# A token tile of 1024 instead of 512, weights always cast on load, and a sample group kept feature-major, in one decoder step on eight cores

## The chip, the cores and the metric

The kernel runs on all 8 cores of one Trainium2 chip (two dies of four cores). Each core does the same program on its own share of the batch; there is no traffic between cores. The metric is the device time of the slowest core in microseconds (us). Executions of one kernel mostly agree within 0.3% (12 of the 15 runs of the kernel before lie that near to their median, and all 8 of the changed kernel); now and then a die falls into a slower state, at a lower granted TensorE clock (in a run of the kernel before that took 1528.1 us, 0.88 on the cores of one die against 0.97 on the other; no trace of a slow run was kept).

## The reference, cut to what matters

One decoder layer with width 1024, for two groups of tokens that use the same weights: a prompt group (per core 1 sequence of 2048 tokens) and a sample group (per core 16 sequences of 4 tokens, so 64 tokens, each sequence with its own recurrent state of 4 x 128 x 256 floats and its own cached keys and values of 256 memory tokens).

```python
def token_mix(xn, s0, buf, pos0, p):
    proj = xn @ p['w_in']
    q, k, v, gz, og, u, ga, gb = jnp.split(proj, split_points(), axis=-1)
    ...
    o, s_new = gla_chunked(q, k, v, log_a, s0)            # gated linear attention with a carried state
    o = rmsnorm(o, p['gla_norm_g']).reshape(B, T, GLA_VAL_W) * jax.nn.silu(og)
    branch_a = o @ p['w_branch_a']
    pooled, buf_new = pool_mix(u, buf, pos0, p['w_pool_mix'], p['pool_scale'])
    branch_b = pooled @ p['w_branch_b']
    merged = jax.nn.sigmoid(ga) * branch_a + jax.nn.sigmoid(gb) * branch_b
    return merged @ p['w_out'], s_new, buf_new

def decoder_layer(x, mk, mv, s0, buf, pos0, p):
    mix, s_new, buf_new = token_mix(rmsnorm(x, p['norm_mix_g']), s0, buf, pos0, p)
    h = x + mix
    h = h + cross_attn(rmsnorm(h, p['norm_x_g']), mk, mv, p['w_xq'], p['w_xo'])
    h = h + sq_relu_mlp(rmsnorm(h, p['norm_mlp_g']), p['w_up'], p['w_down'])
    return h, s_new, buf_new
```

All inputs are float32. The kernel's matmuls take bf16 operands.

## The kernel before: the parts that matter

The program is written as a list of operations per engine, which a scheduler in the kernel orders at build time. Weights come in units of 1024 x 512 (1 MB in bf16), each landing in a slot. `W(name)` hands out the next slot and starts its load: from the float32 weights with a cast on the way, or, where the same unit has been cast before, from a bf16 scratch in HBM.

```python
NSLOT = 5
NT = SEQ // 512                                  # four prompt tiles of 512 tokens
...
def W(self, name):
    ...
    if name in ONCE:
        cast, store = True, False
    elif name[:2] == "bp":
        cast, store = False, False
    elif times <= STORE_AT.get(name, 1):
        cast, store = True, times == STORE_AT.get(name, 1)
    else:
        cast, store = False, False
    if cast:
        self.dma("pool", flat, src, nb=5.0, ahead=60.0, after=...)
    else:
        self.dma("sp", flat, self.scr[idx], nb=2.5, rtok=[("scr", idx)], ahead=60.0)
    if store:
        self.dma("sp", self.scr[idx], flat, nb=2.5, wtok=[("scr", idx)])
    return u
```

The prompt is done tile by tile; each stage of a tile asks for a unit and uses it on all the tile's tokens. The sample group's 64 tokens are done beside it, whenever a unit that they need is in a slot, and in generators that the prompt's loops step forward (`self.step("G", 2)`). Two projections exist: `sfm` holds the weights still and streams 64 tokens, `stm` holds the tokens still and streams 512 weight columns.

```python
def sfm(self, u, srcT):                          # 32 matmuls of 64 columns
    b = self.bank()
    self.mms([(self.pb[b][:, m * 64:(m + 1) * 64], self.fm(u, m, srcT, 64)) for m in range(4)])
def stm(self, u, srcT):                          # 8 matmuls of 512 columns
    b = self.bank()
    self.mm(self.pb[b][:64, :], self.tm(u, 0, srcT, sp=64))
```

The carried states of the 16 sequences go through a ring of buffers. To get one sequence's four query rows against its own state while keeping 64 output rows, the queries sit in a window of zeros (`qw`):

```python
for i in range(SB):
    sf = self.ring(...)                                                    # float32 state
    self.dma("sp", sf[...], I["sgla"][i], nb=1.4)
    self.cp("act", sb_[:, :, :], sf[:, :, :])                              # bf16 copy, ScalarE
    self.cp("dve", qw[:, :, 60:64], self.qs[:, :, i * ST:(i + 1) * ST])
    self.ts("dve", kb[:, :], self.kdts[:, :], self.bmk[:, i:i + 1], ALU.mult, ...)
    for hp in range(2):
        self.mma([(self.pb[ob[hp]][:64, ...], [(qw[:, h, 60 - ST * i:124 - ST * i], sb_[:, h, :])]) for h in ...], ...)
        ...                                                                # state update, 64-row operands
    self.dma("sp", O["sgs"][i], sf[...], nb=1.4)
```

Of the kernel before, what the change touches and what calls it, by code (L numbers as in the profile page):

```python
# [19 lines left out]
SB = 16  # L20
# [4 lines left out]
NSLOT = 5  # L25
NT = SEQ // 512
# [416 lines left out]
def make_consts():  # L443
# [26 lines left out]
    mu = np.zeros((64, 4, 64), np.float32)  # L470
# [17 lines left out]
    bk = np.zeros((64, SB), np.float32)  # L488
# [9 lines left out]
for _n, _w in (("g_mix", 8), ("g_x", 8), ("g_mlp", 8), ("g_mem", 8), ("g_gla", 2), ("pscale", 8), ("bgk", 4)):  # L498
    COLS[_n] = (_o, _w)
    _o += _w  # L500
# [21 lines left out]
ONCE = ("xk0", "xk1", "xv0", "xv1", "b0", "b1", "xqT0", "xqT1", "xq0", "xq1", "xo0", "xo1")  # L522

STORE_AT = {f"up{i}": 0 for i in range(8)}
STORE_AT.update({f"dn{c}_{n}": 0 for c in range(4) for n in range(2)})
STORE_AT.update(dict.fromkeys(("og0", "og1", "u0", "u1"), 2))
# [15 lines left out]
class Fixed:  # L542
    def __init__(self, ap):
        self.ap = ap

# [12 lines left out]
class Prog:  # L558
    def __init__(self):
        self.nc = nc = bass.Bass("TRN2", target_bir_lowering=False)  # L560
# [9 lines left out]
        inp("xp", [SEQ, D]); inp("xs", [SB * ST, D]); inp("mem", [MEM, D])  # L570
# [6 lines left out]
        outp("yp", [SEQ, D]); outp("ys", [SB * ST, D]); outp("mk", [MEM, D]); outp("mv", [MEM, D])  # L577
# [3 lines left out]
        with contextlib.ExitStack() as stack:  # L581
# [3 lines left out]
            self.mark = {}  # L585
            for mode in ("count", "plan", "emit"):
# [22 lines left out]
                self.seen = {}  # L609
# [14 lines left out]
    def alloc(self):  # L624
# [5 lines left out]
        def reg(size, gran=256):  # L630
# [6 lines left out]
        self.ur = g.sb("ur", reg(10240), [128, 5, 1024], BF16)  # L637
        self.WqK = g.sb("WqK", reg(16384), [128, 8, 1024], BF16)
        self.VWo = g.sb("VWo", reg(16384), [128, 8, 1024], BF16)
        self.wt += [g.sb(f"wx{i}", g.byname[n] + o, [128, 8, 512], BF16)  # L640
                    for i, (n, o) in enumerate((("WqK", 0), ("WqK", 8192), ("VWo", 0), ("VWo", 8192)))]
        XH = reg(16384)
        self.xh = g.sb("xh", XH, [128, 4, 1024], F32)
        self.actT = g.sb("actT", reg(8192), [128, 8, 512], BF16)
        R = reg(16384)
        self.E1 = g.sb("E1", R, [128, 4, 512], F32)
        self.E2 = g.sb("E2", R + 8192, [128, 4, 512], F32)
        self.o2T = g.sb("o2T", R, [128, 8, 512], BF16)
        self.dT = g.sb("dT", R + 8192, [128, 8, 512], BF16)
        self.hid = [g.sb(f"hid{i}", R + 8192 * i, [128, 8, 512], BF16) for i in range(2)]  # L650
        Q = reg(24576)
        self.qi = g.sb("qi", Q, [128, 4, 512], BF16)
        self.kd = g.sb("kd", Q + 4096, [128, 4, 512], BF16)
        self.kdt = [g.sb(f"kdt{i}", Q + 8192 + 1024 * i, [128, 512], BF16) for i in range(2)]
        self.Sb = [g.sb(f"Sb{i}", Q + 10240 + 2048 * i, [128, 4, 256], BF16) for i in range(2)]
        self.T1 = g.sb("T1", Q, [128, 4, 512], F32)
        self.vt = g.sb("vt", Q + 14336, [128, 4, 1024], BF16)
        self.att = [g.sb(f"att{i}", Q + 22528 + 1024 * i, [128, 4, 128], BF16) for i in range(2)]
        self.mT = g.sb("mT", Q, [128, 8, 512], BF16)
        self.t1 = g.sb("t1", Q + 8192, [128, 4, 512], F32)  # L660
        self.t2 = g.sb("t2", Q + 16384, [128, 4, 512], F32)
        self.Pn = [g.sb(f"Pn{i}", Q + 8192 + 2048 * i, [128, 4, 256], BF16) for i in range(4)]
        self.PT = [g.sb(f"PT{i}", Q + 16384 + 2048 * i, [128, 8, 128], BF16) for i in range(4)]
        self.land = [g.sb(f"land{i}", Q + 4096 * i, [128, 1024], F32) for i in range(4)]
        UR = g.byname["ur"]
        self.s0m = [g.sb(f"s0f{i}", o, [128, 4, 256], F32) for i, o in enumerate((Q + 16384, Q + 20480, UR, UR + 6144))]
        self.s0a = [g.sb(f"s0g{i}", XH + 4096 * i, [128, 4, 256], F32) for i in range(4)]
# [3 lines left out]
        self.junk = g.sb("junk", reg(2048), [128, 1024], BF16)  # L671
        self.ogs = [g.sb(f"ogs{i}", R + 8192 + 2048 * i, [128, 1024], BF16) for i in range(4)]
        self.memT = g.sb("memT", XH, [128, 8, 256], BF16)
        self.Mtm = [g.sb(f"Mtm{i}", XH + 4096, [128, 2, 1024], BF16) for i in range(2)]
        self.mstage = [g.sb(f"mstage{i}", XH + 8192 + 2048 * i, [128, 512], F32) for i in range(4)]
        X = reg(26624, 64)
        self.xsh = g.sb("xsh", X, [64, 1024], F32)
        self.xns = g.sb("xns", X + 4096, [64, 1024], BF16)
        self.acs = g.sb("acs", X + 6144, [128, 8, 64], BF16)
        self.dTs = g.sb("dTs", X + 7168, [128, 8, 64], BF16)  # L680
        self.o2s = g.sb("o2Ts", X + 8192, [128, 8, 64], BF16)
        self.ustage = [g.sb(f"ustage{i}", X + o, [64, 512], F32) for i, o in enumerate((7168, 4096))]
        Y = X + 9216
        self.Ps = g.sb("Ps", Y, [128, 4, 64], F32)
        self.E1s = g.sb("E1s", Y + 1024, [128, 4, 64], F32)
        self.kds = g.sb("kds", Y + 2048, [128, 4, 64], BF16)
        self.qs = g.sb("qs", Y + 2560, [128, 4, 64], BF16)
        self.kps = g.sb("kps", Y + 3072, [128, 4, 64], BF16)
        self.atts = g.sb("atts", Y + 3584, [64, 4, 64], BF16)
        self.kdts = g.sb("kdts", Y + 4096, [64, 512], BF16)  # L690
        self.vts = g.sb("vts", Y + 5120, [64, 1024], BF16)
        self.ogss = g.sb("ogss", Y + 7168, [64, 1024], BF16)
        self.qwin = [g.sb(f"qwin{i}", Y + 9216 + 1024 * i, [128, 4, 124], BF16) for i in range(2)]
        self.s0b = [g.sb(f"s0b{i}", Y + 11264 + 2048 * i, [128, 4, 256], BF16) for i in range(2)]
        self.kblk = [g.sb(f"kblk{i}", Y + 15360 + 1024 * i, [64, 512], BF16) for i in range(2)]
        self.urs = g.sb("urs", Y + 11264, [64, 1024], BF16)
        self.uh = g.sb("uh", Y + 13312, [120, 2, 1024], BF16)
        self.mTs = g.sb("mTs", Y, [128, 8, 64], BF16)
        self.t1s = g.sb("t1s", Y + 1024, [128, 4, 64], F32)
        self.t2s = g.sb("t2s", Y + 2048, [128, 4, 64], F32)  # L700
        self.qxs = g.sb("qxs", Y + 2048, [128, 8, 64], BF16)
        self.PTs = g.sb("PTs", Y + 3072, [128, 8, 64], BF16)
        self.oxs = g.sb("oxs", Y + 4096, [128, 8, 64], BF16)
        self.xwin = [g.sb(f"xwin{i}", Y + 5120 + 1984 * i, [128, 8, 124], BF16) for i in range(2)]
        self.Pns = g.sb("Pns", Y + 5120, [64, 4, 256], BF16)
        kv = [g.sb(f"kv{i}", Y + 9216 + 4096 * i, [128, 2048], BF16) for i in range(2)]
        self.kvm = kv + [g.sb(f"km{i}", o, [128, 2048], BF16) for i, o in enumerate((Q + 16384, Q + 20480, UR + 4096))]
        self.kva = kv + [g.sb(f"va{i}", XH + 4096 * i, [128, 2048], BF16) for i in range(4)]
        self.hids = g.sb("hids", Y + 9216, [128, 32, 64], BF16)
        self.meml = g.sb("meml", XH + 8192, [128, 2, 1024], F32)  # L710
        self.pmf = g.sb("pmf", X + 8192, [128, 2048], F32)
        self.pmT = g.sb("pmT", X + 16384, [128, 8, 256], BF16)
        self.KT = g.sb("KT", X + 20480, [128, 8, 256], BF16)
        self.VT = g.sb("VT", X + 16384, [128, 8, 256], BF16)
        self.bpt = [g.sb(f"bpt{i}", X + 8192 * i, [128, 8, 512], BF16) for i in range(2)]
# [8 lines left out]
        self.ident = small("ident", [128, 128], BF16)  # L724
        self.maskT = small("maskT", [128, 128], BF16)
# [5 lines left out]
        self.smu = small("smu", [64, 4, 64], BF16)  # L731
        self.bmk = small("bmk", [64, SB], F32)
# [4 lines left out]
        self.gzT = small("gzT", [16, 512], BF16)  # L737
        self.gzs = small("gzs", [16, 64], BF16)
        self.eB = [small(f"eB{i}", [128, 4, 4], F32) for i in range(2)]
        self.eBs = small("eBs", [128, 4, 16], F32)  # L740
        self.r3 = small("r3", [128, 4, 4], F32)
# [24 lines left out]
    def W(self, name):  # L766
        k = self.ninst
        self.ninst += 1
        u = Unit(self, name, k)
        if self.mode == "count":  # L770
            self.inst.append([name, self.g.n, self.g.n])
            return u
        s = self.slot[k]
        idx = UNITS[name][0] if name in UNITS else UNITS["b" + name[2]][0]
        g = self.g
        times = self.seen.get(name, 0)
        self.seen[name] = times + 1
        dst = self.wt[s]
        flat = dst[:, :, :].rearrange("p k n -> p (k n)")
        src = self.I["wu"][idx]  # L780
        if name in ONCE:
            cast, store = True, False
        elif name[:2] == "bp":
            cast, store = False, False
# [8 lines left out]
        if store:  # L793
            self.dma("sp", self.scr[idx], flat, nb=2.5, wtok=[("scr", idx)])
# [1075 lines left out]
```

## Time and profile before

| | before |
|---|---|
| median time, 15 runs beside the changed kernel | 1429.3 us |
| profiled run, slowest core | 1428.0 us |
| TensorE busy | 1321.0 us |
| matmuls, columns streamed (instruction listing) | 7976, 2,978,304 |
| changes between a full and a partly used array (listing) | 203 |
| mean granted clock of the cores | 0.962 to 0.969 |

In the profile's lines PE is TensorE, PEld its weight loads, DVE VectorE, ACT ScalarE, POOL GpSimd and SP the engine whose queue issues the plain DMAs; L825 is line 825 of the kernel, and `out<-in` names buffers: wt a weight slot, wu the float32 weights, xh the running activations, xn their normed copy, s0f a sample state and s0b its bf16 copy, kv and va the cached keys and values. A hole is time in which TensorE waits. The granted clock is the share of full TensorE speed that the profile shows as given; the bill is the time that the matmuls would need without holes at full clock.

The lines that carry the main reading are in the prediction below. Beside them, these lines of the page of the kernel before show the weight traffic: bytes to and from HBM, then the issues with size and the median time from issue to landing.

```profile
HBM read 289.73 MB, written 56.36 MB: 242 GB/s over the span
...
wt<-wscratch SPq DMA_DIRECT2D x82, 1024.0 KB, 5.7
wt<-wu POOLq DMA_DIRECT2D x60, 1024.0 KB, 21.8
wscratch<-wt SPq DMA_DIRECT2D x32, 1024.0 KB, 23.3
```

The reader is to see that a casting load (wt<-wu) takes four times as long to land as a scratch load (21.8 us against 5.7; most casts, 52 of the 60, are issued in the first 551 us, and the mean DMA share is 0.96 up to 44 us, 0.94 from there to 365 and 0.93 on to 620, so this is not the cost of the cast alone), and that 32 MB are written to HBM only to be read back.

### The profile page before, as it was taken

Reading aid. Unit: us, or ns where it says so; the run is one execution under the profiler, and the core shown is the slowest. Engines: PE = TensorE matmul, PEld = TensorE weight load, DVE = VectorE, ACT = ScalarE, POOL = GpSimd, SP = SyncE. Lnnn points to the kernel's source line nnn. Section 1 sums busy time; section 2 is a strip of 40 time slices with the busy share of each in tenths; the row PEclk is TensorE's granted clock in tenths of the full one; section 3 lists DMA queues with packets and bytes.
Section 4 is the critical chain, followed back from the end, with each engine's and each line's share of the span. In section 5 each row is a group of like instructions: output and inputs, shape, how many; then the busy total and the mean of one; then the engine's idle time right before and its main releaser. Section 6 shows DMA issues by size and latency. Waiting matters only on the chain.

```text
span 1428.0 us, 22529 instructions; the slowest of 8 cores (1411.6 to 1428.0 us)
## 1 busy us (share of the span) xinstructions
PE 1321.0 (93%) x7976; PEld 655.3 (46%) x7976; DVE 660.8 (46%) x1115; ACT 649.0 (45%) x1359; POOL 61.1 (4%) x117
## 2 busy tenths in 40 slices
PE   5998993999899699999998899999999989999997
PEld 3455441544335353554444455554444544455443
DVE  3564331653545232554584642563445532364445
ACT  3574343731155463852233775672115546573112
POOL 3000000000000000000000000000010100000000
PEclk7999896999999899999999899999999989999999
DMA  9999997789999999654579735638399894532331
GB/s 203 166 167 172 171 195 143 243 165 208 218 207 223 184 226 259 217 177 148 195 272 239 239 118 189 160 81 247 121 208 227 233 218 164 151 116 87 121 119 67
DMA packets 46809, 259.35 MB, mean 182 GB/s; under 512 B 6022, under 2 KB 6478, under 8 KB 23260
## 3 DMA queue, kind: packets, MB, share of 16 engines
q0 software_dynamic: 16160, 89.58, 39.1%
q1 hardware_dynamic: 30540, 168.33, 34.6%
q8 instruction: 66, 1.08, 0.3%
q14 instruction: 43, 0.35, 0.1%
HBM read 289.73 MB, written 56.36 MB: 242 GB/s over the span
## 4 chain that ended last, share of the span: by engine, by line
PE 69%; DMA 25%; issue 1%; DVE 1%; ACT 1%; SPq 1%; another core or an unknown queue 1%; DVEq 0%; ACTq 0%; POOLq 0%
PE pb L825 61%; DMA wt<-wu 9%; DMA wscratch<-wt 6%; PE pb L836 4%; DMA xh<-xp 3%; PE pb L855 2%; DMA va<-cv 2%; DMA wt<-wscratch 2%; PE pb L846 2%; DMA s0f<-sgla 1%; DMA kv<-ckT 1%; DMA land<-xp 1%; DMA sgs<-s0f 1%; SPq L926 1%
## 5 line engine op out<-in xcount | busy, mean ns | idle before, releaser
L825 PE MATMUL pb<-actT,wt 128*128 128x512 bf16 (+2 forms) x1920 | 399.8, 366 | 12.3 <-DMA wt<-wu 8.8
L825 PEld LDWEIGHTS pb<-actT,wt 128*128 128x128 bf16 x1920 | 180.1, 98 | 214.2 <-issue 19.7
L825 PE MATMUL pb<-wt,hid 128*128 128x512 bf16 x1024 | 231.9, 383 | 7.9 <-DMA wt<-wu 7.5
L874 ACT ACTIVATE tmp<-pb 128x512 f32<-128x512 f32 (+1 forms) x172 | 98.9, 585 | 240.9 <-PE pb L825 205.6
L825 PE MATMUL pb<-wt,actT 128*128 128x512 bf16 x704 | 170.6, 399 | 16.9 <-DMA wt<-wu 16.5
L825 PEld LDWEIGHTS pb<-wt,hid 128*128 128x128 bf16 x1024 | 97.9, 98 | 129.2 <-issue 19.6
L897 DVE SCALAR_TENSOR_TENSOR xh<-pb,r,xh 128x512 f32<-128x512 f32 x128 | 95.9, 750 | 115.8 <-PE pb L825 115.0
L897 DVE SCALAR_TENSOR_TENSOR hid<-pb,tmp 128x512 bf16<-128x512 f32 x128 | 86.8, 689 | 113.0 <-ACT tmp L874 112.9
L874 ACT ACTIVATE xn<-xh 128x512 bf16<-128x512 f32 (+1 forms) x81 | 56.0, 703 | 163.9 <-DVE xh L897 90.2
L825 PEld LDWEIGHTS pb<-wt,actT 128*128 128x128 bf16 x704 | 69.1, 101 | 103.3 <-issue 35.2
L886 DVE TENSOR_TENSOR t<-t,pb 128x512 f32<-128x512 f32 x64 | 44.0, 687 | 124.5 <-PE pb L825 89.2
L886 DVE TENSOR_TENSOR xh<-pb,xh 128x512 f32<-128x512 f32 x64 | 42.9, 688 | 79.6 <-PE pb L825 49.5
L855 PE MATMUL pb<-ident,xn 128*128 128x128 bf16 x512 | 40.7, 226 | 33.6 <-ACT xn L874 23.4
L926 POOL DMA_DIRECT2D wt<-wu x60 | 32.2, 537 | 912.2 <-PE pb L836 369.5
L874 ACT ACTIVATE t<-pb 128x512 f32<-128x512 f32 x64 | 37.7, 589 | 63.9 <-PE pb L825 63.5
L825 PE MATMUL pb<-WqK,actT 128*128 128x512 bf16 x256 | 58.0, 379 | 1.0 <-ACT actT L874 1.0
L825 PE MATMUL pb<-VWo,PT 128*128 128x512 bf16 x256 | 58.0, 379 | 0.0
L825 PE MATMUL pb<-wt,mT 128*128 128x512 bf16 x256 | 57.8, 384 | 0.0
L825 PE MATMUL pb<-o2T,wt 128*128 128x512 bf16 x256 | 56.6, 379 | 0.0
L855 PEld LDWEIGHTS pb<-ident,xn 128*128 128x128 bf16 x512 | 34.6, 101 | 46.6 <-issue 36.7
L874 ACT ACTIVATE t<-t,ncols 128x512 f32<-128x512 f32 x64 | 46.1, 720 | 3.7 <-ACT t L874 0.4
L825 PE MATMUL pb<-dT,wt 128*128 128x512 bf16 x192 | 44.1, 390 | 3.5 <-DMA wt<-wscratch 3.5
(231 smaller groups left out, 1486.8 us busy)
## 6 DMA issues: line engine op xcount, KB each, us to landing
wt<-wscratch SPq DMA_DIRECT2D x82, 1024.0 KB, 5.7
wt<-wu POOLq DMA_DIRECT2D x60, 1024.0 KB, 21.8
wscratch<-wt SPq DMA_DIRECT2D x32, 1024.0 KB, 23.3
land<-xp SPq DMA_DIRECT2D x16, 512.0 KB, 11.8
xh<-xp SPq DMA_DIRECT2D x16, 512.0 KB, 32.2
yp<-xh SPq DMA_DIRECT2D x15, 512.0 KB, 37.3
s0f<-sgla SPq DMA_DIRECT2D x15, 512.0 KB
sgs<-s0f SPq DMA_DIRECT2D x15, 512.0 KB, 5.2
```

The lines of the kernel that those rows point to most:

```text
L825: ins = e.matmul(out, l, r, start=(start and i == 0), stop=(stop and i == m - 1))
L836: ins = e.matmul(out, l, r, start=(i == 0), stop=(i == m - 1))
L846: ins = e.matmul(out, l, r, start=False, stop=last and k == len(al) - 1)
L855: ins = e.transpose(o, i, d)
L874: return self.g.op("act", lambda e: e.activation(out=out, in_=in_, func=func, scale=scale, **kw), reads=rd, writes=wr, cost=c)
L886: return self.g.op(eng, lambda e: e.tensor_tensor(out=out, in0=in0, in1=in1, op=op), reads=[in0, in1], writes=[out], cost=self.vcost(eng, ...
L897: return self.g.op(eng, lambda e: e.scalar_tensor_tensor(out=out, in0=in0, scalar=scalar, in1=in1, op0=op0, op1=op1), reads=rd, writes=[ou ...
L926: return self.g.op(q, lambda e: e.dma_start(out=out, in_=in_), reads=[in_], writes=[out], cost=0.6 if q == "pool" else 0.07, dma=True, nb= ...
```

## The change

The intent: use each weight for twice as many tokens, so that fewer loads are needed and the scratch is not; and keep the sample group's tensors with features on the partitions, so that its tokens are what streams.

```diff
-NSLOT = 5
-NT = SEQ // 512
+NSLOT = 4
+NT = SEQ // 1024
@@ W() @@
-        if name in ONCE:
-            cast, store = True, False
-        elif name[:2] == "bp":
-            cast, store = False, False
-        elif times <= STORE_AT.get(name, 1):
-            cast, store = True, times == STORE_AT.get(name, 1)
-        else:
-            cast, store = False, False
...
+        if name[:2] == "bp":
+            idx = UNITS["b" + name[2]][0]
+            self.dma("sp", flat, self.scr[idx], nb=2.5, rtok=[("scr", idx)], ahead=60.0)
         else:
+            self.dma("pool", flat, self.I["wu"][UNITS[name][0]], nb=5.0, ahead=60.0, after=...)
@@ sample group: output gate, out-projections, MLP down, as features x tokens @@
-                b = self.stm(u, X)
+                b = self.sfm(u, X)
...
@@ states() @@
-            self.cp("dve", qw[:, :, 60:64], self.qs[:, :, i * ST:(i + 1) * ST])
+            self.mmx([(self.pb[ob][:, j * 64 + i * ST:j * 64 + (i + 1) * ST], sb_[:, j // 2, (j % 2) * 128:(j % 2 + 1) * 128],
+                       self.qs[:, j // 2, i * ST:(i + 1) * ST], False, i == SB - 1 and j == 7) for j in range(8)])
...
-                self.mma([(self.pb[ob[hp]][:64, (h % 2) * 256:(h % 2 + 1) * 256],
-                           [(qw[:, h, 60 - ST * i:124 - ST * i], sb_[:, h, :])]) for h in (2 * hp, 2 * hp + 1)], i == SB - 1)
@@ operands of the sample group padded with zero rows to the full array @@
-        self.vts = g.sb("vts", Y + 5120, [64, 1024], BF16)
+        self.vts = g.sb("vts", Y + 7168, [128, 1024], BF16)
@@ pooling: what the previous block gives streams 16 columns instead of 128 @@
-                    pairs = [(self.ur[:, pr, csl], self.pm01[:, 1, g, :]), (self.ur[:, cu, csl], self.pm01[:, 0, g, :])]
+                        items += [(o, l, self.pm01[:, 0, g, :], True, False),
+                                  (self.pb[b][:, s4 * 128:s4 * 128 + 16], self.ur[:, pr, csl], self.pm01[:, 1, g, :16], False, True)]
```

Cuts are marked with dots; "@@" lines name the place. The rest of the change is the new layout of on-chip memory (buffers of 1024 tokens take the room of the lent weight slots), doubled loops over two halves of 512 columns, and the placing of the sample group's steps.

## The prediction

Its bill takes 2400 columns a us and 2.5 ns a matmul. Both are estimates from the trace of the kernel before, in which the median from start to next start, between matmuls of one shape on the full array, is 216 ns at 512 columns, 109 at 256, 56 at 128 and 29 at 64: (216 - 29) / (512 - 64) = 0.417 ns a column, so some 2400 a us, which leaves 2.3 to 2.7 ns a matmul at the four sizes. The 25 ns at four columns is measured; that sixteen columns also take 25 ns was an estimate (26 ns measured in the changed kernel). The price of 6.2 us is that of a casting load: q0 is the queue that POOL issues to, and all wt<-wu are on it. In the 20 us window of the long hole (220 to 240 us, TensorE busy 0.10 us) the granted clock is 0.50.

> **What bounds the kernel now.** I read the cores first (all eight within 1411.6 to 1428.0 us, both dies alike, so the state is fast), then the totals and the slices of the page, then TensorE's waits, then its timeline in several stretches.
>
> ```profile
> PE 1321.0 (93%) x7976; PEld 655.3 (46%) x7976; DVE 660.8 (46%) x1115; ACT 649.0 (45%) x1359; POOL 61.1 (4%) x117
> PE   5998993999899699999998899999999989999997
> PEclk7999896999999899999999899999999989999999
> DMA  9999997789999999654579735638399894532331
> ...
> q0 software_dynamic: 16160, 89.58, 39.1%
> q1 hardware_dynamic: 30540, 168.33, 34.6%
> ```
>
> TensorE is busy for 93% of the span; VectorE and ScalarE are under half. The digits say when it is not busy: at the start, around slices 5 to 7, 10 to 14, 22 and 33, and in each of these the DMA digit is 9 (or was just before) and the clock digit drops too. The waits put names to it:
>
> ```profile
> PE pb L825 <- DMA wt<-wu: 32.7, 9, 12.0
> PE pb L855 <- ACT xn L874: 23.4, 1, 23.4
> PE pb L855 <- DVE xn L892: 10.2, 3, 4.9
> PE pb L836 <- DMA va<-cv: 6.7, 3, 3.2
> PE pb L836 <- DVE kblk L892: 5.2, 1, 5.2
> PE pb L825 <- DMA wt<-wscratch: 3.5, 1, 3.5
> ```
>
> 32.7 us is the wait for weights that are cast from float32 on the way in. The 23.4 us behind ScalarE is a DMA too: in the chain of waits it is the reload of x into xh, issued at 181 us and landing near 229 us, because the weight traffic (casts, and their bf16 copies written back to HBM) fills the queues. The 10.2 us is the loading of x at the start. The sample group's own loads (va, kv, and kblk, which waits for a state) cost nearly 20 us. So the kernel is bound by TensorE's own streaming, plus DMA holes in the first 512-token tile.
>
> How fast TensorE streams can be read off the timeline (start, duration, group):
>
> ```profile
> 896.65 1.10 PE L836 MATMUL pb<-acs,wt 128*128 128x64 bf16 x32
> 897.58 2.75 PE L825 MATMUL pb<-wt,mT 128*128 128x512 bf16 x12
> ...
> 1135.40 0.54 PE L836 MATMUL pb<-PTs,va 128*128 128x4 bf16 x16
> 1135.80 0.38 PE L836 MATMUL pb<-vt,kdt 128*128 128x256 bf16 x2
> ...
> 677.40 0.41 PE L846 MATMUL pb<-s0b,qwin 128*64 128x256 bf16 x2
> 677.74 0.39 PE L836 MATMUL pb<-vts,kblk 64*128 64x256 bf16 x2
> 678.06 1.90 PE L825 MATMUL pb<-wt,hid 128*128 128x512 bf16 x8
> 679.89 0.41 PE L846 MATMUL pb<-s0b,qwin 128*64 128x256 bf16 x2
> ```
>
> Take start to next start, not the duration[...]. Thirty-two 64-column matmuls take 0.93 us (29 ns each); sixteen 4-column ones 0.40 us (25 ns each); elsewhere eight 512-column ones take 1.73 us (216 ns). The last four lines show a tax: two 256-column matmuls that use only 64 output columns or only 64 rows of the array take 0.34 and 0.32 us where 0.22 is normal (the vt,kdt pair at 75.75 us), and the eight full ones behind them take 1.83 us where 1.73 is normal. Each change between the full array and a half of it costs about 0.1 us.
>
> [...] the clock is 1.00 through 620 to 780 us of unbroken work with all cores running. [...] Its price here: q0's share 39.1% x 1428 / 89.58 MB = 6.2 us per bf16 MB landed, against 34.6% x 1428 / 168.33 = 2.9 us for plain copies.
>
> **The bill of the kernel before.** From its instruction listing: 7976 matmuls, 2,978,304 columns. Columns / 2400 = 1241.0 us; 7976 x 2.5 ns = 19.9; 256 four-column ones raised to 25 ns = 5.3. Sum 1266. Changes of array shape, counted in the listing: 203 x 0.1 = 20. Idle: 1428 - 1321 = 107. Slow clock, from 20 us windows as busy time x (1 - clock): 28. Total 1421 of 1428; 7 unexplained. The bill holds well enough to be applied to the other kernel.
>
> **The change, part by part.** (1) The token tile goes from 512 to 1024, so every weight is used for 64 full matmuls (64 x 0.216 = 13.8 us) instead of 32 (6.9 us) per load. (2) So weights are loaded twice instead of four times, always with the cast: 82 cast loads instead of 66 (wt and wx), and the 82 loads from the bf16 scratch and 34 stores to it shrink to 4 and 2. (3) Weight slots fall from 9 (5 + 4 lent) to 4. (4) The sample group becomes feature-major: weights stand still and its 64 tokens stream, and cache scores and old-state reads stream 4 columns; operands are zero-padded to 128 rows. (5) In pooling the part from the previous block streams 16 columns instead of 128. (6) The sample states move from the second 512-token tile to the gate stage of the first 1024-token tile.
>
> TensorE's bill after, from the listing of the changed kernel (built, not run): 8421 matmuls, 2,889,600 columns. 1204.0 + 21.1 + 640 four-column x 20.8 ns = 13.3 + 120 sixteen-column x 15.8 ns = 1.9; sum 1240. That is 26 less. Its largest terms: 144 sample matmuls of 512 columns become 32 (-24 us) and 448 of 64 columns are added (+13); 128 score matmuls of 256 columns become 256 of 4 (-14, +6.4); 64 state reads of 256 become 128 of 4 (-7, +3.2); pooling -6.7, +3.0. Shape changes: 32 instead of 203, so 3 us instead of 20 (-17).
>
> DMA after: 82 x 1.05 MB x 6.2 = 533 us, kv 16.8 MB x 6.2 = 104, plain copies some 53 MB x 2.9 = 154 (x twice, y, states in and out, small things). Sum 791 us of about 1320, 60% instead of 74%, and it is spread: a unit needs 6.5 us of DMA for 13.8 us of TensorE. Only one stretch stays tight: from the k projection to the fourth chunk of the first tile, 15 units (10 of them for the folded attention and pooling weights, with 3.5 us of matmuls each) and 6 MB of other traffic need 98 + 17 = 115 us of DMA against about 105 of TensorE work.
>
> Losses after, stage by stage, all estimates. Start: before, 44 us had passed when 18.5 us of matmuls were done, so 25.7 lost. After, two x blocks and the first weight come first and each weight serves eight blocks, but 4 MB of x instead of 2 must land; I expect about 55 us for 36 of work: 19. Tight stretch 12. State ring (four buffers; store and reload take some 5 + 10 us against 3 x 6 us of slack) and kv loads 11. ScalarE and VectorE 10: in the first three chunks of a tile ScalarE needs 3 x 1.95 us of sigmoids + 4.8 us against about 8 of TensorE. Slow clock after holes 8. Tail 9, as before (last matmul 1419, end 1428). Unexplained 7. Sum 76.
>
> 1240 + 3 + 76 = 1319; I say 1320, which is -109 us: -26 columns, -17 shape changes, -66 holes, clock and start.
>
> **The rivals.** (a) The casts become the bound: four slots refilled at 6.2 us per MB behind kv loads in one queue, TensorE waiting at each swap. For: median landing was 21.8 us, and a stage that holds two slots has only two ahead. Against: two slots ahead are 27 us of matmuls, and the queue is less full. If it is right, perhaps 68 loads x 1 us: 1390. (b) ScalarE or VectorE becomes the bound: less to hide behind, sigmoids of eight blocks in a row, out-projection and transposes now a loop of their own (ScalarE 4.0 us per block against TensorE's 3.9). Both engines stay near 650 us of 1320, so at most some 30 us locally: 1345. (c) Nothing but the columns counts, since the holes are re-created elsewhere: 1385. (d) Everything hides: losses of 45, 1288. [...]
>
> **Range and chances.** (d) is the low end; the high end has (b) and half of (a): 1370. Being within 2% needs over 1400, so (a) in full and more. Faster 0.94, same 0.05, slower 0.01.
>
> **What would show it.** TensorE busy near 1270 us with the waits for wt<-wu below 15 us and the xh hole gone: the DMA step is right. PTs and qxs matmuls of 4 columns at 25 ns, and full matmuls next to them at 216: the columns and shape steps are right. First 60 us: the k projection starts near 55 us. Wrong: many waits of 1 to 5 us on wt<-wu all along (a), waits on ScalarE or VectorE over 20 us (b)[...].

## The result, and the profile after

The changed kernel took 1313.9 us (median of 8 runs, 1310.2 to 1315.0), correct, against 1429.3 us for the kernel before: a ratio of 0.919, 95% interval 0.9175 to 0.9204. Ratios here and below are the mean time of one kernel's fast runs over that of the other's of the same rounds, so not quite the ratio of the medians. A second set of runs of the changed kernel, on another chip, gave 0.9231 (below), so a ratio carries some 0.004 from set to set, about 6 us. Where an experiment is compared with the changed kernel across sets, I give the range between the two.

The page of the changed kernel, to be held against the same lines in the prediction and above (columns of the first line: busy us, share, instructions; then the busy digits of TensorE, its clock, the DMA share; then queues with packets, MB and share):

```profile
PE 1261.0 (96%) x8426; PEld 642.3 (49%) x8426; DVE 654.8 (50%) x1088; ACT 648.3 (49%) x1333; POOL 68.1 (5%) x131
PE   5998999999979999999999999999999999999997
PEclk7999999999989999999999999999999999999999
DMA  9889986247988946477778659535551313343513
...
q0 software_dynamic: 18112, 104.29, 48.3%
q1 hardware_dynamic: 15452, 55.15, 12.3%
HBM read 241.63 MB, written 22.80 MB: 201 GB/s over the span
...
wt<-wu POOLq DMA_DIRECT2D x82, 1024.0 KB, 11.5
```

TensorE's busy time fell by 60.0 us and the time in which it was not busy from 107 to 51.4 us; together that is the whole gain. The holes of slices 5 to 7, 10 to 14, 22 and 33 are gone; the start, a dip at slice 4 and one notch at slice 12 (361 to 394 us) are left. A casting load now lands in half the time (11.5 us against 21.8), though there are more of them. Why is not shown apart: with the stores alone put back (below) it is 12.4 us against 10.5 in the same set, so the stores by themselves don't explain the 21.8.

TensorE's waits in the changed kernel (us in total, times, longest):

```profile
PE pb L830 <- DVE xn L865: 12.6, 2, 10.2
PE pb L802 <- DMA wt<-wu: 10.4, 3, 5.4
PE pb L821 <- ACT s0b L849: 7.7, 1, 7.7
PE pb L812 <- DMA wt<-wu: 2.1, 1, 2.1
```

The 23.4 us wait behind the reload of xh has no successor. Weights cost 12.5 us in four waits (the second and the last line) instead of 36.2 in ten (32.7 for casts, 3.5 for scratch loads). The wait for s0b has grown from 2.3 us: a state of the sample group arrives late.

TensorE's timeline of the changed kernel around that wait (start, duration, group, idle before):

```profile
373.85 0.35 PE L821 MATMUL pb<-qs,s0b 128*128 128x4 bf16 x8 [7.66 <-ACT s0b L849]
...
385.58 0.34 PE L821 MATMUL pb<-qs,s0b 128*128 128x4 bf16 x8
385.78 0.60 PE L812 MATMUL pb<-vts,kblk 128*128 128x256 bf16 x4
386.21 1.89 PE L802 MATMUL pb<-wt,mT 128*128 128x512 bf16 x8
387.94 0.61 PE L830 MATMUL pb<-ident,xn 128*128 128x128 bf16 x8
```

Start to next start again: eight 4-column matmuls take 0.20 us (25 ns each), four of 256 columns take 0.43 us (108 ns each, where the half-used array before took 160 to 170), and the eight full ones behind them take 1.73 us, not 1.83. Here the sample group's work no longer slows its neighbours.

### The profile page after: what moved, and what is told of

Read it like the earlier page. It is cut to its first block, busy times and chain, and to the rows that moved or that the text cites. A ratio compares the mean times of both kernels' runs of the same rounds, so it can differ in the third digit from the quotient of the medians.

```text
span 1312.4 us, 23088 instructions; the slowest of 8 cores (1295.5 to 1312.4 us)
## 1 busy us (share of the span) xinstructions
PE 1261.0 (96%) x8426; PEld 642.3 (49%) x8426; DVE 654.8 (50%) x1088; ACT 648.3 (49%) x1333; POOL 68.1 (5%) x131
## 3 DMA queue, kind: packets, MB, share of 16 engines
q0 software_dynamic: 18112, 104.29, 48.3%
q1 hardware_dynamic: 15452, 55.15, 12.3%
HBM read 241.63 MB, written 22.80 MB: 201 GB/s over the span
## 4 chain that ended last, share of the span: by engine, by line
PE 85%; DMA 11%; issue 1%; ACT 1%; DVE 1%; POOL 0%; SPq 0%; DVEq 0%; ACTq 0%; POOLq 0%
PE pb L802 76%; DMA wt<-wu 5%; PE pb L812 5%; PE pb L830 3%; DMA kv<-ckT 2%; DMA sgs<-s0f 1%; DMA s0f<-sgla 1%; DMA xsF<-xs 1%; PE pb L821 1%; ACT tmp L849 1%; DVE xn L870 0%; ACT xn L849 0%; DVE xh L870 0%; ACT stat L849 0%; DVE S L870 0%
## 5 line engine op out<-in xcount | busy, mean ns | idle before, releaser
L802 PE MATMUL pb<-actT,wt 128*128 128x512 bf16 x1792 | 402.2, 379 | 3.7 <-DMA wt<-wu 1.9
L849 ACT ACTIVATE tmp<-pb 128x512 f32<-128x512 f32 (+1 forms) x238 | 138.4, 586 | 344.8 <-PE pb L802 305.9
L903 POOL DMA_DIRECT2D wt<-wu x82 | 43.9, 536 | 996.8 <-PE pb L812 426.1
L849 ACT ACTIVATE tmp<-tmp,ncols 128x512 f32<-128x512 f32 x98 | 70.0, 715 | 6.0
L849 ACT ACTIVATE xn<-xh 128x512 bf16<-128x512 f32 (+1 forms) x49 | 36.9, 755 | 61.1 <-DVE xh L870 52.8
L849 ACT ACTIVATE tmp<-tmp 128x512 f32<-128x512 f32 (+2 forms) x103 | 62.3, 607 | 6.4 <-ACT tmp L849 0.4
L859 DVE TENSOR_TENSOR t<-tmp,pb 128x512 f32<-128x512 f32 x32 | 22.0, 688 | 82.7 <-PE pb L802 50.5
L802 PE MATMUL pb<-dT,wt 128*128 128x512 bf16 x256 | 59.0, 379 | 0.0
L859 DVE TENSOR_TENSOR tmp<-tmp,pb 128x512 f32<-128x512 f32 x32 | 22.0, 688 | 57.7 <-PE pb L802 49.2
L859 DVE TENSOR_TENSOR actT<-pb,cols 128x1024 bf16<-128x1024 bf16 x32 | 38.9, 1220 | 8.4 <-PE pb L830 8.1
## 6 DMA issues: line engine op xcount, KB each, us to landing
wt<-wu POOLq DMA_DIRECT2D x82, 1024.0 KB, 11.5
sgs<-s0f SPq DMA_DIRECT2D x16, 512.0 KB, 13.1
```

What stands on the lines that cost most here:

```text
L802: ins = e.matmul(out, l, r, start=(start and i == 0), stop=(stop and i == m - 1))
L849: return self.g.op("act", lambda e: e.activation(out=out, in_=in_, func=func, scale=scale, **kw), reads=rd, writes=wr, cost=c)
L859: return self.g.op(eng, lambda e: e.tensor_tensor(out=out, in0=in0, in1=in1, op=op), reads=[in0, in1], writes=[out], cost=self.vcost(eng, ...
L903: return self.g.op(q, lambda e: e.dma_start(out=out, in_=in_), reads=[in_], writes=[out], cost=0.6 if q == "pool" else 0.07, dma=True, nb= ...
```

## The experiments

Twelve kernels ran, in three sets, each on one chip with the kernel before beside it (medians of before: 1423.4, 1421.3 and 1420.2 us).

### Which part of the kernel gained: the prompt or the sample group?

The sample group was taken out of each kernel. The sample outputs are then not written, so the result is wrong. In the changed kernel:

```diff
-        self.sample_hooks(ti)
...
-            self.sample_in()
...
-            self.hook("pool")
-            self.gen["G"] = self.sample()
```

> The changed kernel without the sample group (its outputs stay unwritten; wrong on purpose). Its TensorE bill, counted as in the prediction, is 1176 us, so 64 us less than with the sample group. Theory (the prompt's part is bare streaming plus a start, a tight stretch and a tail): 1176 + 1 for shapes + 26 start + 13 tight stretch + 8 tail + 8 other = about 1232, so the sample group costs some 80 us. Rival (the sample group hides in holes that the prompt has anyway): 1275 or more.

Measured 1237.5 us, ratio 0.8701 (0.8679 to 0.8723). And in the kernel before:

```diff
-        if ti >= 1:
-            self.sample_hooks(ti)
...
-            self.gen["P"] = self.sample_in()
```

> The kernel before without the sample group (outputs unwritten on purpose). Its bill is 1178 us, the same as the changed kernel's prompt part. Theory A (half of the gain is in the prompt's holes: casts, stores and the late xh in the first tile): 1178 + 2 + 26 start + 60 holes with their slow clock + 9 tail + 8 = about 1283, 50 above the changed kernel without samples. Theory B (all of the gain is the sample group's cheaper matmuls): both prompt-only kernels within 10 us of each other.

Measured 1282.9 us, ratio 0.9012 (0.8987 to 0.9038). TensorE's first waits in the kernel before without its sample group:

```profile
PE pb L825 <- DMA wt<-wu: 21.2, 10, 4.9
...
PE pb L855 <- ACT xn L874: 9.8, 1, 9.8
```

and in the changed kernel without it:

```profile
PE pb L802 <- DMA wt<-wu: 8.1, 2, 4.7
```

What follows. The prompt alone is 45 us faster (1282.9 - 1237.5). Its matmul bill by the prediction's formula is 1178 us in the one and 1176 in the other, so this part is not columns: it is holes, as theory A had it (1283 expected). TensorE's idle time is 68 us in the one and 33 in the other, 13 us of the difference in the waits for weights and 10 in the reload of xh; some 7 us more are slow clock. The sample group costs 140 us in the kernel before (1423.4 - 1282.9), and 71 to 76 us in the changed one (1423.4 x (0.919 to 0.923) - 1237.5; some 80 expected). So of the gain some 45 us come from the prompt and 64 to 70 from the sample group. How much of the latter is matmuls can be read from TensorE's busy time with the slow clock taken off (busy time x (1 - clock) over 20 us windows): the sample group takes 1293 - 1185 = 108 us of it before and 1250 - 1182 = 68 after. These 40 us are the columns and shape changes, where the prediction's bill has 24 + 17; the rest of the sample group's gain, 25 to 30 us, is waits and clock. The parts of the change were not built one by one: what the tile, the missing scratch, the slots and the place of the states each give the prompt is not shown by these two runs.

### Was the scratch worth having in the kernel before?

The kernel before with every unit cast at each use, and no scratch:

```diff
-        elif times <= STORE_AT.get(name, 1):
-            cast, store = True, times == STORE_AT.get(name, 1)
         else:
-            cast, store = False, False
+            cast, store = True, False
```

> The kernel before, with every weight cast from float32 in every tile: no bf16 scratch, 142 casts instead of 66, no 34 stores. Theory (what fills the queues is four loads per weight, so the tile of 1024 is what empties them): DMA share goes up from 74% to about 80%, holes move to the later tiles, 1400 to 1440 us. Rival (the stores to the scratch made the holes; dropping the scratch was the gain, not the larger tile): 1370 or less.

Measured 1454.6 us, ratio 1.0207 (1.0168 to 1.0246), some 29 us slower and above the range that I had given. The rival, that the scratch alone was the trouble, falls. The page shows why: the casting queue moves 169 MB instead of 90, and TensorE's waits keep their two largest entries.

```profile
PE pb L823 <- DMA wt<-wu: 32.0, 10, 6.7
PE pb L853 <- ACT xn L872: 22.0, 1, 22.0
```

With four uses of a weight the scratch pays here; dropping it alone was a loss.

### What would the scratch do in the changed kernel?

Stores of the cast units during the first tile, and loads from the scratch in the second:

```diff
+            if self.ti == 1 and times:
+                self.dma("sp", flat, self.scr[idx], nb=2.5, rtok=[("scr", idx)], ahead=60.0)
+            else:
                 self.dma("pool", flat, self.I["wu"][idx], nb=5.0, ahead=60.0, after=...)
+                if self.ti == 0 and times == 0 and ...:
+                    self.dma("sp", self.scr[idx], flat, nb=2.5, wtok=[("scr", idx)])
```

> The changed kernel with the bf16 scratch put back: 34 more stores in the first tile, 34 plain loads in place of casts in the second. Theory: the first tile's DMA goes from about 75% to 90%, so its two waits for weights grow: 5 to 20 us slower; nothing gained in the second tile, where the casts hide. Rival (casts in the second tile cost something): up to 5 us faster.

Measured 1347.9 us, ratio 0.9471 (0.9432 to 0.951): 0.024 to 0.028 above the changed kernel, so 34 to 40 us slower, nearly twice what I had expected at most (20). That was the largest miss of an expectation so far, and it bears on the question of why the change gains. So the stores were then tried alone, with the condition of the loads set to False, beside a fresh set of runs of the changed kernel itself.

> The changed kernel itself, byte for byte the same instructions, as the yardstick for the other three runs on this chip. Expected 0.919 of the kernel before (0.916 to 0.924), near 1308 to 1314 us, TensorE busy 1261 us within 3 us, one hole of 5 to 10 us before the recurrent-state matmuls of the sample group (ScalarE's s0b cast waiting for the s0f load).

Measured 1309.9 us, ratio 0.9231 (0.9207 to 0.9255); TensorE busy 1263.0 us; the hole in front of the state matmuls is 4.2 us this time, just under the range.

> The changed kernel with the 38 stores of cast weights to a scratch in HBM put back during the first tile, but nothing ever reads them; every load stays a casting load, as in the changed kernel. The earlier run with stores and scratch loads cost about 37 us, most of it seen as a clock of 0.89 to 0.93 between 66 and 420 us and one hole of 14.6 us before s0b. Theory S (the stores do it: 40 MB more traffic in the stretch in which the DMA share is already near 0.9): 25 to 45 us slower than the changed kernel on this chip, clock below 0.95 in the windows up to 260 us, s0b hole over 10 us. Rival L (the scratch loads do it, by their place on the same queue as the activations' loads): under 10 us slower, clock as in the changed kernel.

The "38 stores" in that text is a miscount: the page has 34. Measured 1341.0 us, ratio 0.9457 (0.9432 to 0.9481), 31 us slower than the changed kernel of the same set. Theory S holds in time and in the hole before s0b (11.8 us); of the clock only half of it came true. The windows of the changed kernel in this set (us from the start; length; busy time of TensorE, its weight loads, VectorE, ScalarE, GpSimd; then clock, DMA share, GB/s):

```profile
66.00:160.00 94.00, 88.15 (x568) 46.61 (x567) 54.27 (x86) 54.55 (x108) 5.81 (x11) 0.96 0.86 160
...
340.00:420.00 80.00, 75.75 (x528) 39.92 (x526) 45.04 (x95) 53.22 (x106) 2.72 (x6) 0.98 0.86 226
```

and those of the run with stores:

```profile
66.00:160.00 94.00, 79.48 (x509) 41.88 (x508) 46.21 (x71) 45.35 (x90) 5.31 (x10) 0.93 0.92 184
...
340.00:420.00 80.00, 68.16 (x467) 35.62 (x464) 35.99 (x71) 48.01 (x90) 2.61 (x5) 0.91 0.80 215
```

TensorE is busy 8.7 and 7.6 us less in these two, and at a lower clock. Over the first 700 us, which hold the first tile and all the stores, it is busy 643 us with them and 667 without (the sums of such windows); after that the two kernels run alike (TensorE 97.5 to 100% busy in each window of both from 700 to 1290 us). What follows: the stores alone cost 31 us of the 34 to 40, in the stretches where the DMA share was already 0.86. A rival is that a store keeps its weight slot busy until it has read it, so that it acts like a missing slot. The waits speak against that: those for weights are 8.8 us with the stores and 10.5 without, while others grew: the one in front of the state matmuls from 4.2 to 11.8, and two for the memory's keys and values (Mtm 6.6, mstage 3.3) are new. The last two can be followed back to transfers: the outputs of these keys and values took 26.5 us to land (median) with the stores and 10.6 without, and ScalarE stood 10.5 us before it could reuse their buffer. The cheap loads of the second tile give nothing back, since little waited for DMA there: after 450 us TensorE waits 3.0 us for DMA in the first profile of the changed kernel (1.9 for weights, 1.1 for keys), and 0.4 us in the second.

### Do columns cost what the bill says?

In the sample group's MLP, the matmuls of 64 columns (32 for each unit) were replaced by 8 of 512 columns, which brings the bill from 1240.3 to 1253.0 us. The sample output is wrong.

```diff
+    def swd(self, u, src, k0=0):
+        b = self.bank()
+        self.mm(self.pb[b][:, :], [(src[:, min(k0 + kc, k0 + 6):min(k0 + kc, k0 + 6) + 2, :], u.ap[:, kc, :]) for kc in range(8)])
+        return b
-                b = self.sfm(u, X)
+                b = self.swd(u, X)
-                b = self.sfm(u, self.hids, 8 * c)
+                b = self.swd(u, self.hids, 8 * c)
```

> The changed kernel with the sample group's 16 MLP units streamed as 8 matmuls of 512 columns each instead of 32 of 64 (with 128 output columns, so the array's shape does not change; sample output wrong on purpose). The bill rises from 1240.3 to 1253.0. Theory (TensorE's columns are on the path one for one): 12.7 us slower. Rival (columns hide behind other waits): under 5 us.

Measured 1322.3 us, ratio 0.9311 (0.9288 to 0.9334), so 11 to 17 us above the changed kernel. The added columns arrive in the time in full; none of it hides.

### Does a change of array shape cost 0.1 us?

The zero padding was taken off the sample group's operands, so that they use 64 rows of the array again. Columns stay the same; the listing has 102 shape changes instead of 32.

```diff
-                [(kb[:, h * 128:(h + 1) * 128], self.vts[:, h * 256:(h + 1) * 256])]
+                [(kb[:64, h * 128:(h + 1) * 128], self.vts[:64, h * 256:(h + 1) * 256])]
...
```

(and in the same way for the uses of `atts`, `urs` and the making of `kb`)

> The changed kernel with the sample operands at 64 rows instead of padded to 128. The bill stays at 1240.3, the changes of array shape go from 32 to 102. Theory (0.1 us each): 7 us slower. Rival (shape costs nothing by itself): within 1 us.

Measured 1314.0 us, ratio 0.9254 (0.9232 to 0.9277): 3 to 9 us above the changed kernel. The interval overlaps that of the changed kernel's second set, so the time alone doesn't settle it; TensorE's busy time does, at 1268.2 us against 1261.0 and 1263.0, and with the slow clock taken off at 1256.8 against 1250.3 in both. Seventy changes for 6.5 us is 0.09 us each.

### Is the start held up by the sample group's loads?

In the changed kernel the k projection began at 66.6 us, where I had put 55. TensorE's timeline there shows a wait of 10 us, in which ScalarE stood 8 us in front of the norm of the sample group, whose input landed only at 19 us; the prompt's next block came after it in ScalarE's instructions:

```profile
10.64 0.61 PE L830 MATMUL pb<-ident,xn 128*128 128x128 bf16 x8 [2.46 <-DVE xn L865]
21.41 1.01 PE L830 MATMUL pb<-ident,xn 128*128 128x128 bf16 x8 [10.15 <-DVE xn L865]
```

So the loads of that input and of an identity matrix were put behind the prompt's activations (the same edit for both):

```diff
-        d("sp", self.identF[:], I["c_ident"][:, :])
+        d("sp", self.identF[:], I["c_ident"][:, :], after=self.xld[7:])
```

> The changed kernel with the sample's x and the float32 identity loaded after the prompt's x instead of between its second and third block. ScalarE waited 8 us for the sample's x in the start. Theory (the first weights land near 20.6 us anyway, and that bounds the start): 0 to 4 us faster. Rival (the wait behind the sample's x is the start's loss): 8 to 10 us faster.

Measured 1310.2 us, ratio 0.9231 (0.9209 to 0.9254): equal to the second set of the changed kernel, 0.004 (6 us) above the first. Its timeline settles what the time can't:

```profile
12.79 0.61 PE L830 MATMUL pb<-ident,xn 128*128 128x128 bf16 x8 [2.14 <-DVE xn L865]
17.41 4.86 PE L802 MATMUL pb<-wt,actT 128*128 128x512 bf16 x15 [4.01 <-DMA wt<-wu]
...
68.75 1.67 PE L802 MATMUL pb<-actT,wt 128*128 128x512 bf16 x7 [0.16 <-issue]
```

The long wait is gone, but six of 1.2 to 4.0 us have taken its place, behind x and weights: 13.6 us in all against 13.8 (2.46 + 10.15 + 1.21) in the changed kernel, and the k projection comes at 68.75 us, no earlier. The start is bound by the arrival of x and the first weights, and ScalarE's wait lay beside that.

### How much do the weight slots matter?

```diff
-NSLOT = 4
+NSLOT = 3
```

> The changed kernel with three weight slots instead of four. A cast lands 11.5 us (median) after issue; a unit is 13.8 us of matmuls. Theory (with four slots one unit ahead is always enough, with three there is none in the stages that hold two): 15 to 60 us slower, in waits for wt<-wu. Rival (slots are not what covers the casts): within 5 us.

Measured 1362.8 us, ratio 0.962 (0.957 to 0.9669), 55 to 61 us slower.

```profile
PE pb L802 <- DMA wt<-wu: 31.9, 9, 7.4
```

This is rival (a) of the prediction come true with one slot less: waits for weights in nine places. With one more of another line they make 33.4 us, 21 to 23 more than with four slots, so they are a part of the loss only: TensorE's idle time grew from 46 us (second profile of the changed kernel) to 85, the rest in small waits behind VectorE and ScalarE, and its busy time by 12 us. Five slots were not run.

### Can the new hole in front of the states be closed?

One more empty step after each of the 16 states, so that the ring asks for its loads and stores more slowly:

```diff
             self.dma("sp", O["sgs"][i], sf[:, :, :].rearrange("p h v -> p (h v)"), nb=1.4)
             yield
+            yield
```

> The changed kernel with one more empty step after each of the 16 recurrent states of the sample group, so that the ring of states asks for half as many loads and stores per microsecond. Theory P (the one hole of 7.7 us and about 2 us of clock beside it come from the ring being asked for too fast): 5 to 10 us faster than the changed kernel, hole before s0b under 1 us, the rest of the sample group later by some 50 us and the tail unchanged. Rival M (the hole is the queue's, filled by the next tile's xh loads, and only moves): within 3 us, another hole of 4 us or more with DMA s0f or xh behind it, or a longer tail.

Measured 1329.0 us, ratio 0.9374 (0.935 to 0.9398): 19 us slower than the changed kernel of the same set, where I had expected 5 to 10 us faster, or, by the rival, no change. Theory P falls; of rival M the moved hole came true, but not its size. The timeline of this run shows the hole in front of s0b gone, and another elsewhere, then small ones that the changed kernel doesn't have:

```profile
376.26 1.01 PE L830 MATMUL pb<-ident,xn 128*128 128x128 bf16 x8 [8.35 <-ACT xn L849]
...
480.78 29.46 PE L802 MATMUL pb<-actT,wt 128*128 128x512 bf16 x129 [3.27 <-DMA wt<-wu]
...
662.56 16.69 PE L802 MATMUL pb<-actT,wt 128*128 128x512 bf16 x64 [4.75 <-DMA wt<-wu]
```

The first is the same late state again: here VectorE stood 12 us in front of the masking of the keys (kblk), which in the program waits for the state's load, and the prompt's residual adds behind it, and ScalarE's copies of their result, waited with it. The load that it waited for was issued by 352 us and landed near 374; eight loads of x (4 MB) and the stores of four states were issued between 329 and 358, so I take it that it queued among them. The later ones come from the delay: the loads of cached keys now fall into 448 to 656 us instead of 408 to 613, beside the first weights of the second tile. That these overlaps cause the later waits is read from the times at which the loads are issued; I did not test it apart. Two more things stand in the trace. The wait of 8.35 us is that of the slowest core: on cores 5 and 7, which end at 1301.6 and 1303.0 us, it is 1.1 us or less. And on all eight cores TensorE has some 9.6 us of new waits behind VectorE and ScalarE (xh 2.5, acs 2.5, tmp 2.4, PT 2.2; at most 0.2 us each in the changed kernel of the same set), between 390 and 580 us. So about half of the 19 us is the same on every core and names no load; that it comes from where the delayed steps of the sample group now fall is likely, but not tested.

The same with the later loads at the start:

> The paced kernel with the identity and the sample activations loaded after the last activation load of the first tile, as in the earlier start run. If the two effects are apart and the start's is 2 to 5 us, this is 2 to 5 us faster than the paced kernel, the fastest of all, near 0.911 of the kernel before. Rival: the start is worth nothing (under 1 us), because what it frees is lost again to the wait for the second weight block.

Measured 1331.8 us, ratio 0.9388 (0.9365 to 0.9412): not faster than the paced kernel. The rival of that text holds: the start edit is worth nothing.

No version beat the changed kernel beyond the spread between its two sets.

## Why the prediction was right, point by point

The prediction said 1320 us, 109 us less; measured were 1313.9 us, 115 less.

**Columns and shapes.** Predicted -26 and -17. With the slow clock taken off (28 us before; about 11 after, worked out over 20 us windows in the same way), TensorE's busy time fell from 1292.6 to 1250.3 us, by 42. The two runs that put columns and shape changes back agree in size with their terms (12.7 expected, 11 to 17 found; 7 expected, 6.5 found in busy time). These steps are shown.

**DMA.** Predicted 791 us of DMA work; the two queues' shares, 60.6% of 1312.4 us, make 795. The price of a casting load came out at 48.3% x 1312.4 / 104.29 = 6.1 us per MB landed, as before (5.7 by the page of the second set). So a cast costs here what it reads rather than what it lands: 5.7 to 6.2 us of the 16 engines per bf16 MB landed are 2.9 to 3.1 per float32 MB read, beside 2.9 per MB for plain copies (12.3% x 1312.4 / 55.15). The HBM counter agrees: 2 x 104.29 MB cast, plus the 32 MB that plain copies read (55.15 - 22.80), make 241 of the 241.63 MB.

**Holes, clock and start.** Predicted -66; measured -56 of idle time and -18 of slow clock, so -74 (with the -42 above it is -116, the difference of the two profiled runs). This is the term that was mis-sized, and its parts are:

| loss after, us | predicted | found |
|---|---|---|
| start | 19 | 26 (66.6 us less 40.4 of matmuls by the bill) |
| tight stretch, first tile | 12 | 13 (9 idle, 4 clock) |
| state ring and cached keys | 11 | 11 (7.7 + 1.1 idle, 2 clock) |
| ScalarE and VectorE | 10 | 4 to 5 |
| tail | 9 | 8 |
| slow clock on top | 8 | 0: about 11 in all, within the rows above |
| unexplained | 7 | 8 |

The start gained nothing over the kernel before (25.7 us lost there, 26 here): the same arrival of x and weights binds it, as the run with the later loads shows. So the sign "the k projection starts near 55 us" failed (66.6). What I had too large was the slow clock, which I counted a second time on top of stages whose loss already had it in, and rival (b): no ScalarE or VectorE work held TensorE for more than 0.8 us at a time after the first 100 us, but for the late state. That the total is out by 6 us only is in part luck: the start was 7 us too small, and these two terms some 14 too large. The row of the state ring is luck too: by the prediction's own numbers (15 us of store and reload against 18 of slack) the ring should not have held anything up. Store and reload took 13.1 + 3.5 us (medians), still under 18, and two thirds of the row is one late state.

One reading was too narrow. The prediction put the DMA holes "in the first 512-token tile", which ends near 405 us. The longest wait for weights (12.0 us) ends at 478, and the waits for kblk, va and kv lie between 780 and 1170 us, in later tiles.

**The rivals.** (a), casts as the bound, is what three slots give (+55 us or more), so four are just enough; with them the waits for weights are 12.5 us, under the 15 that I had named. (c), holes re-created elsewhere, came true for one hole of 4 to 8 us only: a late state of the sample group, in the stretch in which x is reloaded. (d), that everything hides, fell: the losses are some 70 us, not 45. The denser stream came with no slow clock: in the profiled run it is 1.00 (0.99 on one core) from 640 to 1300 us, with TensorE busy 653 of these 660 us on the slowest core and 643 or more on every one.

**What the prediction did not see.** It priced the scratch at its bytes and let it vanish into "holes". The run with stores alone shows that 34 MB of stores in the first tile of the changed kernel cost 31 us, two thirds of what the prompt gained (45 us).

## What to carry to other kernels

Bill TensorE by columns, a small fixed cost and the array's shape changes (here, by estimate from the spacing in the trace, 2400 columns a us, 2.5 ns a matmul and 0.1 us a change), and add only the holes of the stages in which DMA is full; that bill fitted both kernels within 8 us. Whether a cache of converted weights in HBM pays depends on the later uses (here it paid some 29 us with four uses of a weight and lost 34 to 40 with two), and its stores must be charged to the stage in which they happen, not to the mean DMA share: here a mean of 60% hid stretches at nearly 90%. An engine that handles both the main work and a side job's late load can pass that lateness on, as VectorE did here (12 us in front of kblk in the paced run, 8.35 us of TensorE's time), so pacing or moving the side job can move a hole instead of closing it.
